# Five reorderings in a two-layer trunk kernel: attention fills, exponentials, query split, last sums, first low parts

## The chip, the cores and the metric

One core of a Trainium2 chip runs the whole kernel in one launch. The metric is the device time of one execution in microseconds; three executions of the kernel before took 386.45, 386.90 and 387.45 us, median 386.9. Below, PE is the matmul engine (TensorE), DVE is VectorE, ACT is ScalarE, POOL is GpSimd and SP is the engine that issues most DMAs.

## The reference

A decoder trunk of two layers over 256 tokens of width 1024, batch 1, all in fp32. Layer 0 is a gated DeltaNet (8 heads); its normalised output feeds shared keys and values and layer 1, a sparse attention with 16 query heads and three branches:

```python
for i in range(N_A_LAYERS):            # layer 0
    x = layer_norm(alpha * x + gated_deltanet_mixer(x, ...))
kv = x @ s_w_kv                        # one shared set: compressed, selected, window
for j in range(N_B_LAYERS):            # layer 1
    q, z, gate = split(x @ b_w_in)     # 1024, 3072, 48 columns
    o_b = softmax(q k_b) v_b           # for each of the three branches b
    y = sum_b sigmoid(gate)_b * o_b * silu(z)_b
    x = layer_norm(alpha * x + y @ b_w_out)
```

With 256 tokens every selection block is taken and the window covers everything, so the two halves of the tokens differ only in how many keys they see.

## The kernel before

Every fp32 product is made of three passes in a rounded fp32 format: high part by high part, high by low, low by high (`fm_part`, L215 to L217; `tm_part`, L233 to L235). The weights come as 512 KB tiles in the order they are used. Each tile is cast to its high part on ACT (L181) and its low part is the difference, on POOL (L185); `presplit` and `get` run some tiles ahead. The names say which weight: `wqkv` is layer 0's input projection, `bq`, `bz` and `bo` are layer 1's query, gate path and output projections; `hi_bz_6` is the high part of the seventh tile of `bz`.

The order of instructions on each engine is the order in which the program writes them: nothing reorders. Three devices set it. `defer(n, f)` puts a piece of work into a list and `step()` emits what has come due. `fills` is a list of small groups of projection matmuls; `fill(n)` takes n of them, so they stand on PE between pieces that wait for other engines. `merges` holds the transposes of finished heads that the output projection reads.

Start (L319 ff.): the tokens' transposed matrix `xT` arrives in four parts. ACT casts a part to `xh`, DVE subtracts for `xl`, and PE multiplies with the first weight chunk, `hi_first` and `lo_first`, whose low parts come from POOL (L322).

Queries: `q_done` rotates a block of queries, `q_split` (L1216) splits it into high and low parts (`hlq`, cast on ACT L1047, difference on DVE L1048), `q_post` transposes on PE into `qtp` and defers the copy to `qT` on ACT (L1224). Two matmul results `gq` give the three gates (`gates`, L1309 ff.: an exponential on ACT, four small instructions on DVE that leave `gt`). `gq` stands in one of the two score banks.

Attention (loop at the end of `trunk`, L1497 ff.): 24 units. A unit of the first token half (t0, named by its first head, such as 012) holds two heads; one of the second half (t1, such as 18) holds one. The string `UNITS` is their order; `FA` and `FB` say how many fill groups stand at two places of each unit. Per unit i: scores on PE; maxima on DVE (at once for t0 units until merges begin, else after `step()`); the copy of the transposed exponentials of the unit before (`probs`, ACT); `step()`, which emits the sums `total` (DVE, L1418 to L1422) and gate paths; FA fills; merges; weight splits; exponentials of unit i on ACT; readout of unit i-1 on PE into an `op` bank; FB fills; transposes of unit i on PE. The gate path of a `bz` block is a tanh on ACT (`th`, L1236) and a product on DVE (`zz`, L1237).

Tail: for the second token half the output projection is made in 256-wide pieces; `done` (L1454) calls `ln_part` (scaled residual plus projection, and statistics, on DVE), then `ln_affine` (L926): mean on DVE, the inverse root on POOL (L922, L923), two affine passes on DVE (L939, L942) and the output DMA.

Of the kernel before, what the change touches and what calls it, by code (L numbers as in the profile page):

```python
# [9 lines left out]
F32 = mybir.dt.float32  # L10
# [3 lines left out]
ALU = mybir.AluOpType  # L14
# [20 lines left out]

FIRST = (1, 2)

UNITS = "001010101101101101111111"
FA = "3113111011210212044211123"
FB = "0211121311122110212111000"  # L40

PRE, TAIL = 4, 2
NEG = -1e30
# [50 lines left out]
def trunk(ctx: ExitStack, tc: tile.TileContext, I: dict, out: bass.AP):  # L94
# [151 lines left out]
    def fill(n, low=True):  # L246
        for _ in range(n):
            step()
            if fills:
                fills.pop(0)()  # L250
            if low:
                lower()
# [66 lines left out]
    def split_first(c):  # L319
        h, l = splits[order[0]]  # L320
        S.copy(h[:, c], first[:, c])
        G.tensor_tensor(l[:, c], first[:, c], h[:, c].bitcast(F32), op=ALU.subtract)  # L322

    splits[order[0]] = tuple(ring.tile([P, 1024], F32R, tag=f"w{i}", name=f"{i}_first", bufs=NSPL) for i in ("hi", "lo"))
    state["s"] = 1
# [3 lines left out]
        PE.matmul(wps[:, 0:256], warm[:, 0:P], warm, start=True, stop=True)  # L329
    ps0 = pjb("pv0")  # L330
    w0 = [i.rearrange("p (k f) -> p k f", k=8) for i in splits[order[0]]]
    for q in range(5):
        if q < 4:
            c = slice(2 * q, 2 * q + 2)
            if q in FIRST:
                split_first(slice(FIRST.index(q) * 512, FIRST.index(q) * 512 + 512))
            for c in [c] if q < 2 else [slice(kt, kt + 1) for kt in (2 * q, 2 * q + 1)]:
                S.copy(xh[:, c, :], xT[:, c, :])
                V.tensor_tensor(xl[:, c, :], xT[:, c, :], xh[:, c, :].bitcast(F32), op=ALU.subtract)
        if q:  # L340
            for kt in range(2 * q - 2, 2 * q):
                for x in (xh, xl):
                    PE.matmul(gps[0:32, T:2 * T], wbs[:, kt, :], x[:, kt, :], start=x is xh and kt == 0,
                              stop=x is xl and kt == 7)
                    PE.matmul(ps0[:, 0:T], w0[0][:, kt, :], x[:, kt, :], start=x is xh and kt == 0, stop=False)
        if q == 2:
            for kt in range(4):
                PE.matmul(ps0[:, 0:T], w0[1][:, kt, :], xh[:, kt, :], start=False, stop=False)
# [559 lines left out]
    def ln_part(t, w, lo, ps, xin, dst):  # L908

        if lo == 0:  # L910
            stt[w, t] = [sm.tile([P, 4, 6], F32, tag="st", name=f"st_{w}{t}"), 0]
        st, n = stt[w, t]
        cc = slice(lo, lo + ps.shape[-1])
        V.scalar_tensor_tensor(dst[:, cc], xin[:, cc], SQRT2, ps, op0=ALU.mult, op1=ALU.add)
        V.bn_stats(st[:, n, :], dst[:, cc])
        stt[w, t][1] += 1

    def ln_mean(t, w):
# [6 lines left out]

    def ln_affine(t, w, b, dst, store=None, src=None):  # L926
        mv = ln_mean(t, w)
        if src:

            for c in range(2):  # L930
                V.scalar_tensor_tensor(src[c], src[c], mv[:, 0:1], lnp[w][:, c * 512:c * 512 + 512],
                                       op0=ALU.subtract, op1=ALU.mult)
            for c in range(2):
                cc = slice(c * 512, (c + 1) * 512)
                V.scalar_tensor_tensor(dst[:, cc], src[c], mv[:, 1:2], lnp[b][:, cc], op0=ALU.mult, op1=ALU.add)
            return
        for c in range(2):
            cc = slice(c * 512, (c + 1) * 512)
            V.scalar_tensor_tensor(dst[:, cc], dst[:, cc], mv[:, 0:1], lnp[w][:, cc], op0=ALU.subtract, op1=ALU.mult)  # L939
        for c in range(2):  # L940
            cc = slice(c * 512, (c + 1) * 512)
            V.scalar_tensor_tensor(dst[:, cc], dst[:, cc], mv[:, 1:2], lnp[b][:, cc], op0=ALU.mult, op1=ALU.add)  # L942
            if store:
                store(cc)
# [313 lines left out]
    add_pairs(48)  # L1258
    S.copy(wgs[:, :, 0:48], wg)
    G.tensor_tensor(wgs[:, :, 48:96], wg, wgs[:, :, 0:48].bitcast(F32), op=ALU.subtract)  # L1260
    fill(1)
    r = q_split()
    fill(1)
    compressed_v()
    for i in range(4):
        if i:
# [115 lines left out]
    def probs(u):  # L1382
        t, h = u
        PT = PTT[u] = wk.tile([P, 2, 2, P], F32, tag="ra", name=f"PT{t}{h}", bufs=6)
        S.copy(PT.rearrange("p a b c -> p (a b c)"), TP[u])  # L1385
        if t == 0 or h % 2:
            h -= h % 2 * t
            PCT[t, h] = pct[len(PCT) % 2]
            S.copy(PCT[t, h][0:32, :], S_[u][0:32, 1, 272:400])
# [53 lines left out]
    def bo_unit(t, c, part):  # L1443
        if part == 0:
            pb_[t, c] = [(sbank(f"pbl{c}{f}")[:, 0] if c else pjb(f"pbl{c}{f}")) for f in range(2)] if t else pjb(f"pbo{c}{t}")
        if t == 0 and c == 1 and part == 1:
            for nm in ("blw", "blb"):
                load_ln(nm, ring.tile([P, D], F32, tag="raw", name=nm, bufs=NRAW))
        x = x1[:, t, :]

        def store(cc):
            nc.sync.dma_start(out[t * P:(t + 1) * P, cc], x[:, cc])

        def done(lo, ps):  # L1454
            ln_part(t, "blw", lo, ps, x, x)
            if lo + ps.shape[-1] == D:
                (ln_affine if t else ln_affine_aside)(t, "blw", "blb", x, store)

        if t == 1:

            for f in range(2):
                ps = pb_[t, c][f][:, 0:256]
                tm_part(ps, ("bo", 4 * c + part), part, t, *bT, cols=slice(256 * f, 256 * f + 256))
                if part == 3:
                    done(512 * c + 256 * f, ps)
            return
        tm_part(pb_[t, c], ("bo", 4 * c + part), part, t, *bT)
        if part == 3:
            defer(1, lambda: done(512 * c, pb_[t, c]))
# [25 lines left out]
    for i in range(n + 1):  # L1495
        if i < n:
            scores(units[i])  # L1497
        first = i < n and units[i][0] == 0 and not merges
        if first:

            maxima(units[i])
        if i:
            probs(units[i - 1])
        step()
        if i < n and not first:
            maxima(units[i])
        fill(int(FA[i]))
        advance()
        presplit()
        if i < n:  # L1510
            exps(units[i])
        if i:
            t, h = units[i - 1]
            if t == 0:
                readout(t, h)
                if h == 14:
                    cnt["t0"] = 1
                    merges += [lambda: merge0(0), lambda: merge0(1)] + ready
            else:

                if (units[i - 2] if h % 2 else units[i]) == (1, h ^ 1):
                    readout(t, h - h % 2, h % 2)
                elif h % 2:
                    readout(t, h - 1)
                if h % 4 == 3:
                    (merges if cnt["t0"] else ready).append(lambda g_=h // 4: merge1(g_))
        fill(int(FB[i]))
        if i < n:
            transposes(units[i])
# [79 lines left out]
```

## Time and profile before

| | |
|---|---|
| median of three executions | 386.9 us |
| the profiled execution | 388.53 us, its span 386.8 us |
| PE busy | 374.7 us, 97% of the span |
| DVE, ACT, POOL busy | 58%, 57%, 64% |
| mean granted PE clock | 0.993 of full |
| chain that ended last | 90% PE, 3% DMA, 2% DVE |

The profile comes from one execution, and its span leaves out 1.7 us of that execution's time. PE's share on the chain says that nearly all of the time is spent with PE at work, so the rows to look for are the few in which PE stands idle and the one that released it.

### The profile page before, as it was taken

To read this page: it belongs to the slowest core of one execution; us is meant where nothing else is said; L and a number is where in the kernel's file an instruction comes from. 1 tells how busy PE (TensorE), PEld (TensorE's weight loads), DVE (VectorE), ACT (ScalarE), POOL (GpSimd) and SP (SyncE) were. 2 spreads that over 40 slices of the span, in tenths; PEclk is the share of its full clock that TensorE was granted. 3 is DMA by queue.
4 is the path that set the end of the run, shared out by engine and by line. 5 is a ranking of instruction groups with operands and counts; after the bars stand their busy time and mean duration, and the time that the engine had idled before them with its cause. 6 is when DMAs were issued, how large, how long until landed. Compare 5 with 4: busy or idle time off the path is not lost.

```text
span 386.8 us, 7558 instructions
## 1 busy us (share of the span) xinstructions
PE 374.7 (97%) x2870; PEld 332.9 (86%) x2870; DVE 223.6 (58%) x591; ACT 220.4 (57%) x433; POOL 247.1 (64%) x157
## 2 busy tenths in 40 slices
PE   8899999999999999999999999999999999999991
PEld 6899999999888987888897878888888888878991
DVE  2777876588642543656542545754557456677726
ACT  4687785546854543535563567675664757456410
POOL 5499999837456747895854997474736547209051
PEclk9999999999999999999999999999999999999997
DMA  6776749845433316384545854433516143301011
GB/s 223 292 218 208 268 158 297 228 167 143 148 109 112 110 54 200 128 287 147 169 158 166 297 195 159 164 111 109 173 45 218 55 153 113 117 3 54 3 54 54
DMA packets 23476, 58.68 MB, mean 152 GB/s; under 512 B 6672, under 2 KB 9232, under 8 KB 23312
## 3 DMA queue, kind: packets, MB, share of 16 engines
q1 hardware_dynamic: 23232, 58.13, 45.1%
q8 instruction: 22, 0.36, 0.4%
q14 instruction: 14, 0.11, 0.1%
q10 hardware_dynamic: 144, 0.07, 0.1%
q0 software_dynamic: 64, 0.01, 0.0%
HBM read 55.96 MB, written 2.23 MB: 150 GB/s over the span
## 4 chain that ended last, share of the span: by engine, by line
PE 90%; DMA 3%; DVE 2%; POOL 1%; ACT 1%; issue 1%; POOLq 0%; SPq 0%; DVEq 0%
PE pbz L235 6%; PE pbz L233 6%; PE pbz L234 6%; PE op L1407 4%; PE s L1336 3%; PE ptp L1378 3%; PE pwz L233 2%; PE pk L217 2%; PE pwo L235 2%; PE pq L216 2%; PE pq L215 2%; PE pq L217 2%; PE pk L215 2%; PE pk L216 2%; PE pwo L234 2%; PE pwo L233 2%
## 5 line engine op out<-in xcount | busy, mean ns | idle before, releaser
L185 POOL TENSOR_TENSOR lo_bz<-raw_bz,hi_bz 128x1024 fp32r<-128x1024 f32 x24 | 56.8, 2392 | 36.2 <-ACT hi_bz L181 19.6
L185 POOL TENSOR_TENSOR lo_wqkv<-raw_wqkv,hi_wqkv 128x1024 fp32r<-128x1024 f32 x22 | 52.5, 2406 | 7.9 <-ACT hi_wqkv L181 6.1
L233 PE MATMUL pbz<-hi_bz,x1h 128*128 128x512 f32 x96 | 38.7, 403 | 0.0
L235 PE MATMUL pbz<-lo_bz,x1h 128*128 128x512 f32 x96 | 37.8, 394 | 0.0
L234 PE MATMUL pbz<-hi_bz,x1l 128*128 128x512 f32 x96 | 37.6, 392 | 0.0
L185 POOL TENSOR_TENSOR lo_bo<-raw_bo,hi_bo 128x1024 fp32r<-128x1024 f32 x8 | 18.9, 2387 | 21.7 <-ACT hi_bo L181 16.9
L185 POOL TENSOR_TENSOR lo_skv<-raw_skv,hi_skv 128x1024 fp32r<-128x1024 f32 x12 | 28.4, 2397 | 4.2 <-PE pskv L235 4.2
L185 POOL TENSOR_TENSOR lo_wz<-raw_wz,hi_wz 128x1024 fp32r<-128x1024 f32 x8 | 19.4, 2438 | 16.0 <-ACT hi_wz L181 10.6
L181 ACT CAST hi_bz<-raw_bz 128x1024 fp32r<-128x1024 f32 x24 | 25.3, 1052 | 2.5 <-POOL wgs L1260 1.6
L185 POOL TENSOR_TENSOR lo_bq<-raw_bq,hi_bq 128x1024 fp32r<-128x1024 f32 x8 | 19.1, 2393 | 11.6 <-ACT hi_bq L181 7.2
L185 POOL TENSOR_TENSOR lo_wo<-raw_wo,hi_wo 128x1024 fp32r<-128x1024 f32 x8 | 18.9, 2385 | 11.9 <-ACT hi_wo L181 11.9
L1385 ACT COPY PT<-ptp 128x512 f32<-128x512 f32 x24 | 14.1, 588 | 21.2 <-PE ptp L1378 21.2
L181 ACT CAST hi_wqkv<-raw_wqkv 128x1024 fp32r<-128x1024 f32 x22 | 22.8, 1043 | 2.4 <-DMA raw_wqkv<-in_wqkv 2.4
L235 PEld LDWEIGHTS pbz<-lo_bz,x1h 128*128 128x128 f32 x96 | 18.0, 188 | 4.3 <-POOL lo_bz L185 0.2
L234 PEld LDWEIGHTS pbz<-hi_bz,x1l 128*128 128x128 f32 x96 | 18.1, 188 | 2.8
L233 PEld LDWEIGHTS pbz<-hi_bz,x1h 128*128 128x128 f32 x96 | 18.1, 188 | 2.8
L1369 ACT ACTIVATE pt<-s,mx 128x256 f32<-128x256 f32 x32 | 13.4, 471 | 10.9 <-DVE mx L1352 8.7
L217 PE MATMUL pk<-xh,lo_wqkv 128*128 128x256 f32 x64 | 18.2, 285 | 0.9 <-POOL lo_wqkv L185 0.9
L215 PE MATMUL pk<-xh,hi_wqkv 128*128 128x256 f32 x64 | 18.6, 290 | 0.0
L215 PE MATMUL pq<-xh,hi_wqkv 128*128 128x256 f32 x64 | 18.5, 289 | 0.0
L216 PE MATMUL pk<-xl,hi_wqkv 128*128 128x256 f32 x64 | 18.1, 283 | 0.0
L217 PE MATMUL pq<-xh,lo_wqkv 128*128 128x256 f32 x64 | 18.1, 283 | 0.0
(362 smaller groups left out, 1257.9 us busy)
## 6 DMA issues: line engine op xcount, KB each, us to landing
raw_bz<-in_bz SPq DMA_DIRECT2D x24, 512.0 KB, 3.3
raw_wqkv<-in_wqkv SPq DMA_DIRECT2D x23, 512.0 KB, 4.4
raw_skv<-in_skv SPq DMA_DIRECT2D x12, 512.0 KB, 3.3
raw_wz<-in_wz SPq DMA_DIRECT2D x8, 512.0 KB, 3.9
raw_wo<-in_wo SPq DMA_DIRECT2D x8, 512.0 KB, 3.6
raw_bq<-in_bq SPq DMA_DIRECT2D x8, 512.0 KB, 3.6
raw_bo<-in_bo SPq DMA_DIRECT2D x8, 512.0 KB, 3.3
raw_w<-in_w SPq DMA_DIRECT2D x4, 512.0 KB, 3.3
```

The lines of the kernel that those rows point to most:

```text
L181: S.copy(h, r)
L185: e.tensor_tensor(l, r, h.bitcast(F32), op=ALU.subtract)
L215: PE.matmul(ps[:, 0:T], wh[:, kt, :], ah[:, kt, :], start=kt == 0, stop=False)
L216: PE.matmul(ps[:, 0:T], wh[:, kt, :], al_[:, kt, :], start=False, stop=False)
L217: PE.matmul(ps[:, 0:T], wl[:, kt, :], ah[:, kt, :], start=False, stop=kt == 7)
L233: PE.matmul(ps, ah[:, kt, tt], wh[:, k4, cols], start=kt == 0, stop=False)
L234: PE.matmul(ps, al_[:, kt, tt], wh[:, k4, cols], start=False, stop=False)
L235: PE.matmul(ps, ah[:, kt, tt], wl[:, k4, cols], start=False, stop=kt == 7)
L1336: PE.matmul(sp[:, j, 0:n], lq, kk[:, hh // 4, c0:c0 + n], start=i == 0, stop=i == 1)
L1369: S.activation(pt[:, :, b, :], s4[:, :, b, :], AF.Exp, bias=mx[:, b:b + 1])
L1385: S.copy(PT.rearrange("p a b c -> p (a b c)"), TP[u])
L1407: PE.matmul(o3[:, r, 1 + b, :], PT[:, j, b, :], vt_[:, b, j, g_, :], start=j == 0, stop=j == 1)
```

## The change

Five parts. (1) `UNITS`, `FA` and `FB` are new tables: the t0 units stand at places 0, 1, 4, 7, 8, 12, 16 and 17 instead of 0, 1, 3, 5, 7, 10, 13 and 16, and the fills are dealt more evenly. (2) In the attention loop the exponentials move up: ahead of `step()` for t0 units until merges begin, and ahead of `presplit()` for the others (one fill group goes behind the merge when there is one). (3) The first `q_split` moves ahead of a fill. (4) In the tail the first half of the second token half's last sums stays in its two PSUM banks; the first affine pass is then three instructions, two of 256 columns from the banks and one of 512. (5) The two low parts of the first chunk move from POOL to DVE, between the subtractions for `xl`.

```diff
--- before.py
+++ after.py
@@ -35,9 +35,9 @@
 
 FIRST = (1, 2)
 
-UNITS = "001010101101101101111111"
-FA = "3113111011210212044211123"
-FB = "0211121311122110212111000"
+UNITS = "001101100111011100111111"
+FA = "3112121111111111111222223"
+FB = "0111111111111111101001000"
 
 PRE, TAIL = 4, 2
 NEG = -1e30
@@ -319,7 +319,8 @@
     def split_first(c):
         h, l = splits[order[0]]
         S.copy(h[:, c], first[:, c])
-        G.tensor_tensor(l[:, c], first[:, c], h[:, c].bitcast(F32), op=ALU.subtract)
+
+        return lambda: V.tensor_tensor(l[:, c], first[:, c], h[:, c].bitcast(F32), op=ALU.subtract)
 
     splits[order[0]] = tuple(ring.tile([P, 1024], F32R, tag=f"w{i}", name=f"{i}_first", bufs=NSPL) for i in ("hi", "lo"))
     state["s"] = 1
@@ -329,14 +330,17 @@
         PE.matmul(wps[:, 0:256], warm[:, 0:P], warm, start=True, stop=True)
     ps0 = pjb("pv0")
     w0 = [i.rearrange("p (k f) -> p k f", k=8) for i in splits[order[0]]]
+    low_first = []
     for q in range(5):
         if q < 4:
             c = slice(2 * q, 2 * q + 2)
             if q in FIRST:
-                split_first(slice(FIRST.index(q) * 512, FIRST.index(q) * 512 + 512))
+                low_first.append(split_first(slice(FIRST.index(q) * 512, FIRST.index(q) * 512 + 512)))
             for c in [c] if q < 2 else [slice(kt, kt + 1) for kt in (2 * q, 2 * q + 1)]:
                 S.copy(xh[:, c, :], xT[:, c, :])
                 V.tensor_tensor(xl[:, c, :], xT[:, c, :], xh[:, c, :].bitcast(F32), op=ALU.subtract)
+            if q % 2:
+                low_first.pop(0)()
         if q:
             for kt in range(2 * q - 2, 2 * q):
                 for x in (xh, xl):
@@ -911,8 +915,9 @@
             stt[w, t] = [sm.tile([P, 4, 6], F32, tag="st", name=f"st_{w}{t}"), 0]
         st, n = stt[w, t]
         cc = slice(lo, lo + ps.shape[-1])
-        V.scalar_tensor_tensor(dst[:, cc], xin[:, cc], SQRT2, ps, op0=ALU.mult, op1=ALU.add)
-        V.bn_stats(st[:, n, :], dst[:, cc])
+        y = ps if dst is None else dst[:, cc]
+        V.scalar_tensor_tensor(y, xin[:, cc], SQRT2, ps, op0=ALU.mult, op1=ALU.add)
+        V.bn_stats(st[:, n, :], y)
         stt[w, t][1] += 1
 
     def ln_mean(t, w):
@@ -925,7 +930,7 @@
 
     def ln_affine(t, w, b, dst, store=None, src=None):
         mv = ln_mean(t, w)
-        if src:
+        if src and not store:
 
             for c in range(2):
                 V.scalar_tensor_tensor(src[c], src[c], mv[:, 0:1], lnp[w][:, c * 512:c * 512 + 512],
@@ -934,9 +939,11 @@
                 cc = slice(c * 512, (c + 1) * 512)
                 V.scalar_tensor_tensor(dst[:, cc], src[c], mv[:, 1:2], lnp[b][:, cc], op0=ALU.mult, op1=ALU.add)
             return
-        for c in range(2):
-            cc = slice(c * 512, (c + 1) * 512)
-            V.scalar_tensor_tensor(dst[:, cc], dst[:, cc], mv[:, 0:1], lnp[w][:, cc], op0=ALU.subtract, op1=ALU.mult)
+        for c, y in enumerate(src):
+            cc = slice(c * 256, (c + 1) * 256)
+            V.scalar_tensor_tensor(dst[:, cc], y, mv[:, 0:1], lnp[w][:, cc], op0=ALU.subtract, op1=ALU.mult)
+        cc = slice(512, 1024)
+        V.scalar_tensor_tensor(dst[:, cc], dst[:, cc], mv[:, 0:1], lnp[w][:, cc], op0=ALU.subtract, op1=ALU.mult)
         for c in range(2):
             cc = slice(c * 512, (c + 1) * 512)
             V.scalar_tensor_tensor(dst[:, cc], dst[:, cc], mv[:, 1:2], lnp[b][:, cc], op0=ALU.mult, op1=ALU.add)
@@ -1258,9 +1265,8 @@
     add_pairs(48)
     S.copy(wgs[:, :, 0:48], wg)
     G.tensor_tensor(wgs[:, :, 48:96], wg, wgs[:, :, 0:48].bitcast(F32), op=ALU.subtract)
-    fill(1)
     r = q_split()
-    fill(1)
+    fill(2)
     compressed_v()
     for i in range(4):
         if i:
@@ -1452,9 +1458,14 @@
             nc.sync.dma_start(out[t * P:(t + 1) * P, cc], x[:, cc])
 
         def done(lo, ps):
-            ln_part(t, "blw", lo, ps, x, x)
+
+            inb = t == 1 and lo < 512
+            ln_part(t, "blw", lo, ps, x, None if inb else x)
             if lo + ps.shape[-1] == D:
-                (ln_affine if t else ln_affine_aside)(t, "blw", "blb", x, store)
+                if t:
+                    ln_affine(t, "blw", "blb", x, store, [p[:, 0:256] for p in pb_[1, 0]])
+                else:
+                    ln_affine_aside(t, "blw", "blb", x, store)
 
         if t == 1:
 
@@ -1501,14 +1512,19 @@
             maxima(units[i])
         if i:
             probs(units[i - 1])
+        if first:
+            exps(units[i])
         step()
         if i < n and not first:
             maxima(units[i])
-        fill(int(FA[i]))
+
+        k = 1 if merges else 0
+        fill(int(FA[i]) - k)
         advance()
+        fill(k)
+        if i < n and not first:
+            exps(units[i])
         presplit()
-        if i < n:
-            exps(units[i])
         if i:
             t, h = units[i - 1]
             if t == 0:
```

The number of instructions stays the same on PE, ACT and SP; DVE gets four more and POOL one row fewer.

ACT at the split of the first query block, before (`hlq000` is the high part of the first block's first half, `kh` the compressed keys', `wgs` the gate weights):

```order
L1259 CAST wgs_2832<-wg_2360 128x8x48 [waits DMAHW2_49]
L1188 CAST kh_2288<-kcp_2825 128x4x16 [waits DVE_49]
L181 CAST hi_bq_7_2846<-raw_bq_7_2737 128x1024 [waits DMAHW6_49,Pool_49]
L181 CAST hi_bz_0_2852<-raw_bz_0_2739 128x1024 [waits DMAHW7_49,Pool_49]
L1047 CAST hlq000_2862<-pbq00_2705 128x4x64
L181 CAST hi_bz_1_2883<-raw_bz_1_2745 128x1024 [waits DMAHW0_49,Pool_49]
```

and now:

```order
L1266 CAST wgs_2832<-wg_2360 128x8x48 [waits DMAHW2_49]
L1054 CAST hlq000_2836<-pbq00_2705 128x4x64 [waits DVE_49]
L1195 CAST kh_2288<-kcp_2825 128x4x16 [waits DVE_49]
L181 CAST hi_bq_7_2849<-raw_bq_7_2737 128x1024 [waits DMAHW6_49,Pool_49]
L181 CAST hi_bz_0_2855<-raw_bz_0_2739 128x1024 [waits DMAHW7_49,Pool_49]
L181 CAST hi_bz_1_2883<-raw_bz_1_2745 128x1024 [waits DMAHW0_49,Pool_49]
```

The cast of `hlq000` moved up past the keys' cast and two weight casts.

ACT at the opening of the attention, before (`qT1` are the last two copies of transposed queries, `gq` the gates' exponential, `pt00` and `Pc00` the exponentials of the first unit, `th00` the tanh of the first gate block):

```order
L181 CAST hi_bz_6_3049<-raw_bz_6_2908 128x1024 [waits DMAHW5_49,Pool_49]
L1224 CAST qT1_2696<-qtp110_3059 128x4x128 [waits PE_49]
L1224 CAST qT1_2696<-qtp111_3064 128x4x128 [waits PE_49]
L1310 ACT_TABLE_LOAD
L1310 ACTIVATE gq_3069<-gq_3069 128x96 [waits PE_49]
L181 CAST hi_bz_7_3090<-raw_bz_7_2935 128x1024 [waits DMAHW6_49,Pool_49]
L1236 ACTIVATE th00_3101<-pbz00_3004 128x512 [waits PE_49]
L1365 ACTIVATE pt00_3117<-s00_3072,mx00_3077 128x128 [waits DVE_49,Activation_49]
L1365 ACTIVATE pt00_3117<-s00_3072,mx00_3077 128x128
L1366 ACTIVATE Pc00_3118<-s00_3072,mx00_3077 128x16
```

and now:

```order
L181 CAST hi_bz_6_3049<-raw_bz_6_2908 128x1024 [waits DMAHW5_49,Pool_49]
L1371 ACT_TABLE_LOAD [waits DVE_49,PE_49]
L1371 ACTIVATE pt00_3081<-s00_3072,mx00_3077 128x128 [waits Activation_49]
L1371 ACTIVATE pt00_3081<-s00_3072,mx00_3077 128x128
L1372 ACTIVATE Pc00_3082<-s00_3072,mx00_3077 128x16
L1371 ACTIVATE pt00_3081<-s00_3072,mx00_3077 128x128 x2
L1372 ACTIVATE Pc00_3082<-s00_3072,mx00_3077 128x16
L1231 CAST qT1_2696<-qtp110_3059 128x4x128
L1231 CAST qT1_2696<-qtp111_3064 128x4x128
L1316 ACTIVATE gq_3069<-gq_3069 128x96
L181 CAST hi_bz_7_3098<-raw_bz_7_2935 128x1024 [waits DMAHW6_49,Pool_49]
```

The table load and the six exponentials of unit 00 moved ahead of both copies and of the gates' exponential; the load now waits for DVE and PE.

DVE around the maxima `mx014` of the last t0 unit, before (`op` and `rc` of one number are one sum, `total`):

```order
L1349 TENSOR_TENSOR s18_3968<-s18_3968,cb_2284 128x256 [waits PE_49,Activation_49]
L1350 TENSOR_TENSOR s18_3968<-s18_3968,cb_2284 128x16 [waits DVE_49]
L1351 TENSOR_REDUCE mx18_3976<-s18_3968 128x2 [waits DVE_49]
L1352 TENSOR_REDUCE mx18_3976<-s18_3968 128x1
L1237 SCALAR_TENSOR_TENSOR zz3_3808<-th41_3993,pbz41_3896 128x512 [waits Activation_49]
L1345 TENSOR_TENSOR s014_4030<-s014_4030,cb_2284 128x2x272 [waits PE_49]
L1346 TENSOR_REDUCE mx014_4035<-s014_4030 128x4 [waits DVE_49]
L1347 TENSOR_REDUCE mx014_4035<-s014_4030 128x2
L1418 RECIPROCAL op16_4014<-op16_4014 128x6
```

and now:

```order
L1351 TENSOR_TENSOR s012_3962<-s012_3962,cb_2284 128x2x272 [waits PE_49,Activation_49]
L1352 TENSOR_REDUCE mx012_3967<-s012_3962 128x4 [waits DVE_49]
L1353 TENSOR_REDUCE mx012_3967<-s012_3962 128x2
L1244 SCALAR_TENSOR_TENSOR zz1_3560<-th50_3982,pbz50_3878 128x512 [waits Activation_49]
L1424 RECIPROCAL op18_3945<-op18_3945 128x6 [waits PE_49]
L1425 TENSOR_TENSOR rc18_4003<-op18_3945,gt_2977 128x6 [waits DVE_49]
L1426 TENSOR_TENSOR op18_3945<-op18_3945,zz3_3869 128x6x64 [waits DVE_49]
L1427 TENSOR_TENSOR op18_3945<-op18_3945,rc18_4003 128x6x64 [waits DVE_49]
L1428 TENSOR_REDUCE zz3_3869<-op18_3945 128x128 [waits DVE_49]
L1351 TENSOR_TENSOR s014_4021<-s014_4021,cb_2284 128x2x272 [waits PE_49]
L1352 TENSOR_REDUCE mx014_4026<-s014_4021 128x4 [waits DVE_49]
L1353 TENSOR_REDUCE mx014_4026<-s014_4021 128x2
```

Before, a gate product stood directly ahead of `mx014`; now a gate product and the five instructions of the sum of 18 do, and the maxima of 012 stand ahead of those.

## Rows read from the trace of the kernel before

**Rows 1.** The page, part 1: busy time of each engine, share of the span, instructions.
```profile
PE 374.7 (97%) x2870; PEld 332.9 (86%) x2870; DVE 223.6 (58%) x591; ACT 220.4 (57%) x433; POOL 247.1 (64%) x157
```

**Rows 2.** Waits of TensorE: line waited for, total us, times, longest.
```profile
PE pk L217 <- POOL lo_wqkv L185: 0.9, 1, 0.9
...
PE qtp L1223 <- DVE hlq L1048: 0.5, 1, 0.5
```

**Rows 3.** Timeline of PE, opening: start us, us, instruction [idle before <-releaser].
```profile
240.28 0.37 PE L1336 MATMUL s<-kh,qT 128*128 128x272 f32 x1
...
240.87 0.40 PE L233 MATMUL pbz<-hi_bz,x1h 128*128 128x512 f32 x1
...
244.98 0.60 PE L1378 MATMUL ptp<-ident,pt 128*128 128x128 f32 x4
...
245.45 0.37 PE L1336 MATMUL s<-kh,qT 128*128 128x272 f32 x1
```

**Rows 4.** Timeline of PE, last attention units.
```profile
337.56 0.91 PE L1378 MATMUL ptp<-ident,pt 128*128 128x128 f32 x4
...
340.02 2.00 PE L1407 MATMUL op<-vtok,PT 128*128 128x65 f32 x16 [0.16 <-DVE zz L1422]
...
344.59 1.11 PE L1407 MATMUL op<-vtok,PT 128*128 128x65 f32 x8 [0.39 <-DVE zz L1422]
```

**Rows 5.** Timeline of DVE after the last matmul.
```profile
380.39 1.42 DVE L939 SCALAR_TENSOR_TENSOR x<-x,mv_blw,blw 128x512 f32<-128x512 f32 x2
382.26 1.42 DVE L942 SCALAR_TENSOR_TENSOR x<-x,mv_blw,blb 128x512 f32<-128x512 f32 x2 [0.46 <-POOL mv_blw L923]
```

**Rows 6.** Chain of waits, 0 to 20 us: start us, us, what.
```profile
6.78 7.41 DMA raw_wqkv<-in_wqkv
...
15.34 2.40 POOL lo_wqkv L185
```

**Rows 7.** Chain of waits, 218 to 246 us.
```profile
221.55 1.06 ACT hi_bz L181
```

**Rows 8.** Timeline of ACT, opening of the attention.
```profile
239.68 1.07 ACT L1224 CAST qT<-qtp 128x512 fp32r<-128x512 f32 x2 [0.20 <-PE qtp L1223]
240.78 1.28 ACT L1310 ACT_TABLE_LOAD   x1
242.07 0.23 ACT L1310 ACTIVATE gq<-gq 128x96 f32<-128x96 f32 x1
...
243.16 0.60 ACT L1236 ACTIVATE th<-pbz 128x512 f32<-128x512 f32 x1
243.64 0.63 ACT L1365 ACTIVATE pt<-s,mx 128x128 f32<-128x128 f32 x2
...
244.30 0.65 ACT L1365 ACTIVATE pt<-s,mx 128x128 f32<-128x128 f32 x2
```

**Rows 9.** Timeline of DVE, opening of the attention.
```profile
241.07 0.73 DVE L1345 TENSOR_TENSOR s<-s,cb 128x544 f32<-128x544 f32 x1 [2.56 <-PE s L1336]
...
242.55 0.26 DVE L1311 TENSOR_SCALAR gq<-gq 128x96 f32<-128x96 f32 x1
...
243.93 0.24 DVE L1315 TENSOR_SCALAR gt<-gq,cb 128x16 f32<-128x16 f32 x1
```

**Rows 10.** Timeline of DVE, last attention units.
```profile
337.18 0.69 DVE L1237 SCALAR_TENSOR_TENSOR zz<-th,pbz 128x512 f32<-128x512 f32 x1 [0.50 <-ACT th L1236]
337.78 0.20 DVE L1418 RECIPROCAL op<-op 128x6 f32<-128x6 f32 x1
...
339.41 0.56 DVE L1422 TENSOR_REDUCE zz<-op 128x128 f32<-128x384 f32 x1
```

**Rows 11.** Timeline of DVE, layer norm of the first layer.
```profile
155.67 1.42 DVE L931 SCALAR_TENSOR_TENSOR pwo<-pwo,mv_alw,lna 128x512 f32<-128x512 f32 x2
157.00 1.40 DVE L935 SCALAR_TENSOR_TENSOR x<-pwo,mv_alw,lna 128x512 f32<-128x512 f32 x2
```

**Rows 12.** Slice 381 to 382 us: busy of each engine, then granted clock.
```profile
381.00:382.00 1.00, 0.00 (x0) 0.00 (x0) 0.80 (x2) 0.00 (x0) 0.92 (x2) 0.82 0.00 0
```

## Prediction

> **What bounds the kernel now.** I read the page first, then what TensorE waits for, then the timelines of the three places the diff touches. TensorE (PE) is busy 374.7 of 386.8 us [rows 1]: anything that lets it start its next matmul earlier is worth its full length, anything that makes it wait costs its full length, and work on the other engines is free until PE stands. So the change can only remove waits of PE and the little that lies before its first and behind its last matmul, and has to be searched for waits it adds.
>
> The waits there are few. Near the start PE waits 0.9 us for one low part of a weight, ahead of the attention 0.5 us for the low part of the split queries [rows 2]. In the attention opening PE runs eighteen fill matmuls behind the first scores, then transposes, then the second unit's scores, without a gap [rows 3]. At the end of the attention it does stand: 0.16 and 0.39 us for the last step of a sum, and the four transposes that need 0.60 us in the opening take 0.91 there [rows 3, 4], because their second pair waits for an exponential. Counting such excess start to start, at some ten places of the same kind between 333.9 and 344.6 us, I get 2.1 us, of which these three rows show 0.9. After the last matmul Vector finishes the layer norm alone [rows 5].
>
> **Part 5, the start: 0.** With the low parts of the first chunk off POOL, the subtractions of x no longer share time with it and PE meets its early matmuls some tenths sooner. But the next thing PE needs is the low part of a projection weight: its DMA takes 7.41 us and lands at 14.19, ACT casts, POOL subtracts from 15.34 for 2.40 [rows 6]. None of the three is moved, so PE arrives sooner and waits longer than 0.9. Bounds: a gain of at most 0.9 would need the transfer to land earlier, and no DMA is issued earlier; a loss would need Vector's extra 1.3 us of subtraction to delay something. I take 0, with ±0.3.
>
> **Part 3, the queries' split: −0.54.** ACT casts hi_bz_0 for 1.06 us [rows 7] directly ahead of the first hlq, and PE then waits 0.5 (0.54 in its row's idle time) for Vector's half of that split [rows 2]. Now the cast of hlq stands two weight casts earlier, behind wgs; its input is long there. The wait goes. Next in line behind it are the matmuls of the query projection, whose weights are split already. What is pushed back 0.27 us is the key cast and two weight casts, consumed over 2 us later. Bounds: 0 to −0.6.
>
> **Part 2 in the opening: +2.70.** Here the move costs. In the row order ACT now does, behind the first maxima: table load, six exponentials of unit 00, then the two last qT copies, then the gates' exponential gq. Before, both copies and gq stood ahead. Nothing else on ACT can pass the table load, since it carries the wait. With the durations of [rows 8] and the times of [rows 3, 9]:
> - The maxima hand over at about 242.6 (the next Vector instruction starts at 242.55 [rows 9]). Before, the table load (1.28) had run from 240.78 beneath the copies' and maxima's time; now it starts at 242.65 and ends at 243.95.
> - Exponentials of a two-head unit take 1.31 from the first start to the last end (243.64 to 244.95): 245.26. The copies take 1.07: 246.33.
> - The transposes of unit 00 take the one transpose bank, which the second copy frees: 246.37 instead of 244.98, a wait of 1.39.
> - gq takes 0.23 and ends near 246.47. Vector's four gate instructions last 1.62 (242.55 to 244.17) and end at 248.1. The second unit's scores need the score bank in which gq stands (two banks, three users), so they start near 248.15 instead of 245.45 [rows 3].
>
> Thus PE stands 1.39 ahead of the transposes and 1.31 behind them, 2.70 in all. Nothing covers it: PE runs in order, and the eighteen matmuls that could have filled it are already spent at 244.98. Bounds: 1.4 if the gates end with the transposes, 2.9 with semaphore delays added.
>
> **Parts 1 and 2 in the rest: −2.1 and +3.0.** The new tables deal one or two fill groups (six matmuls, 4.11/3 = 1.37 us) to every unit, and leave no late unit without. The excess at the end goes: I count all 2.1 as gained. But they also move two-head units (t0) together to places 16 and 17, with only one group and one readout between the scores of the last, unit 014, and its transposes. Walk that place from the scores of 012 at time 0. Maxima start at +0.79 and take 1.55 (241.07 to the next row) [rows 9]; exponentials start a tenth later, at 2.46, and the next ACT work, th50, at 3.78 (0.60 [rows 8], its reader Vector released after 0.6). Then Vector runs zz50 (0.6 to its successor [rows 10]), then the sum of 18, 337.78 to 339.97 or 2.19 [rows 10], and only then the maxima of 014: near 7.2. Those give 8.75, exponentials end near 10.2. PE meanwhile: scores 0.58, group, readout 1.04, group, transposes 0.47, scores 0.58, group, readout 1.04, which is 7.8 (scores and transposes from [rows 3]; a readout is the 1.11 of [rows 4] less what lies under its successor). It waits some 2.3; I take 1.9, since a few of these ends overlap their successors' starts by a tenth. The same walk at the other units gives 0.43 (a readout behind the sum two units back), 0.3 (maxima behind a zz), 0.37 (a copy behind two weight casts) and 0.6 (exponentials behind a copy of merged heads, a th and a cast), rounded together to 3.0 after 0.6 off for those that a wait just before already covers. Bounds: 0.8, if Vector is ahead at each place because PE was held just before, to 4.5.
>
> **Part 4, the tail: −0.5.** Today Vector's first affine pass reads and writes SBUF and the second starts 1.87 us after it (380.39 to 382.26), held 0.46 by POOL's power [rows 5]. In the first layer's norm, whose operand lies in PSUM, the same pair stands 1.33 apart and POOL is no wait [rows 11]. Two of the three new instructions read PSUM, so I expect that distance and a little more, for the third instruction: 1.37, a gain of 0.5. Bounds 0 to −0.55. The sums and statistics of the first half move to PSUM in equal number and size: the 512-wide affine pair takes 1.42 from PSUM as from SBUF [rows 5, 11], so no price. [...]
>
> **Sum.** +2.70 +3.0 −0.54 −2.1 −0.5 +0 = **+2.6 us**. The profiled execution took 388.53 (span 386.8), 1.6 over the median of 386.9; added to its own time the sum gives 391.1, and against the median, which is what is forecast, **389.5 us**. A measurement of this kernel tells about 0.3% (1.16 us) from no change.
>
> **Rivals.**
> - *Only the opening costs.* The late chains bind little (0.8) because Vector and ACT run ahead: 2.70+0.8−3.14 = +0.4, **387.3 us**, no change. For it: Vector is idle 42% of the span [rows 1]. Against it: at unit 014 the order itself serializes zz, sum and maxima, whatever the idle share.
> - *Faster.* The table load's wait isn't what it seems, or gq's bank is not what holds the second scores, so that the opening costs 1.4 at most and the late waits 0.5: 1.9−3.14 = −1.2, **385.7 us**. It decides when opening and late waits together stay under 3.14 − 1.16 = 1.98 us. Against it: two independent orders, ACT's and the bank's, would both have to be misread.
> - *The clock falls in the opening.* PE would stand 1.39 us, do 0.47 of transposes and stand 1.31. [...] Against it: the transposes break the stand into two, and no row shows the clock falling before PE's last matmul, though no wait there is longer than 0.9 [rows 2]. [...]
>
> **Chances and range.** Forecast (+1.2 to +4.4) 0.72, only the opening 0.15, clock 0.08, faster 0.05. So slower 0.80, no change 0.15, faster 0.05. The range runs from 387.2 (late waits at their lower bound) to 391.3 (late waits at 4.5 with the gains short by a little), leaving out the faster case, the clock case and a strip of each end.
>
> **What would show it.** In the new profile: the table load near 242.1 on ACT (0.54 earlier than above) with the copies and gq behind the exponentials; PE idle about 1.4 ahead of the first transposes, released by ACT's copy, and about 1.3 ahead of the second scores, released by Vector's gates; a wait near 2 us of the transposes of 014 on an exponential; no wait for hlq; an unchanged arrival of lo_wqkv near 17.7; the last pair of affine passes about 1.4 apart. The prediction is wrong if PE's waits behind the opening come to less than 1 us in total, or if the second scores don't wait.

## The result and the profile after

The changed kernel took 391.81 us in the median of six executions (390.02 to 396.58), the kernel before 387.02; the ratio is 1.0117 (95% interval 1.0077 to 1.0156), some 4.5 us. The forecast was 389.5 with a range that ended at 391.3: the direction was right, the size nearly twice as large, and the time lies outside the range. The shortest executions lie half a microsecond over the sum; it is the others, up to 6 us longer, that carry the median out. The longest counts as a slow execution, which the ratio leaves out; the median of the other five is 391.19, but three more runs of the same kernel, below, gave 391.75 to 392.32.

TensorE's work is the same, so its busy time hardly moved (before: [rows 1]):

```profile
PE 375.3 (97%) x2870; PEld 332.3 (86%) x2870; DVE 223.2 (57%) x594; ACT 219.2 (56%) x433; POOL 243.9 (63%) x155
```

Its waits, as in [rows 2] (line waited for, total us, times, longest):

```profile
PE ptp L1384 <- ACT qT L1231: 1.4, 1, 1.4
PE s L1342 <- DVE gt L1321: 1.1, 1, 1.1
...
PE op L1410 <- DVE zz L1428: 0.8, 2, 0.4
PE ptp L1384 <- ACT pt L1371: 0.5, 1, 0.5
PE gps L372 <- DVE ba L357: 0.4, 1, 0.4
```

The wait for hlq is gone, and so, here, is that for the first low weight. New are the two of the opening, the second query copy (1.4) and the gates (1.1). The place itself, on PE, and what ACT did (before: [rows 3, 8]):

```profile
238.00 0.37 PE L1342 MATMUL s<-kh,qT 128*128 128x272 f32 x1
...
244.22 0.66 PE L1384 MATMUL ptp<-ident,pt 128*128 128x128 f32 x4 [1.35 <-ACT qT L1231]
...
246.12 0.36 PE L1342 MATMUL s<-kh,qT 128*128 128x272 f32 x1 [1.13 <-DVE gt L1321]
```

```profile
240.44 1.28 ACT L1371 ACT_TABLE_LOAD   x1 [3.23 <-DVE mx L1353]
...
243.06 1.11 ACT L1231 CAST qT<-qtp 128x512 fp32r<-128x512 f32 x2
244.01 0.30 ACT L1316 ACTIVATE gq<-gq 128x96 f32<-128x96 f32 x1
```

```profile
245.74 0.24 DVE L1321 TENSOR_SCALAR gt<-gq,cb 128x16 f32<-128x16 f32 x1
```

ACT loads its table at 240.44, when the maxima are there, works through the exponentials, copies the queries at 243.06 and does gq at 244.01, as the new order says; Vector's last gate instruction ends at 245.98, and the second scores start at 246.12. From first to second scores PE takes 8.12 us where it took 5.17 [rows 3]: +2.95.

At unit 014 the chain of Vector that the prediction walked stands in the trace, a product, the sum of 18, then the maxima (before: [rows 9, 10]):

```profile
329.80 0.69 DVE L1244 SCALAR_TENSOR_TENSOR zz<-th,pbz 128x512 f32<-128x512 f32 x1 [2.11 <-ACT th L1243]
330.41 0.20 DVE L1424 RECIPROCAL op<-op 128x6 f32<-128x6 f32 x1
...
332.51 0.72 DVE L1351 TENSOR_TENSOR s<-s,cb 128x544 f32<-128x544 f32 x1
...
333.88 0.18 DVE L1353 TENSOR_REDUCE mx<-s 128x2 f32<-128x32 f32 x1
```

```profile
332.74 1.08 PE L1410 MATMUL op<-vtok,PT 128*128 128x65 f32 x8 [0.37 <-DVE zz L1428]
...
334.60 1.27 PE L1384 MATMUL ptp<-ident,pt 128*128 128x128 f32 x4 [0.50 <-ACT pt L1371]
```

The product starts at 329.80, the sum at 330.41, the maxima at 332.51, and the transposes that need the exponentials start 0.50 late and take 1.27 instead of 0.60: 1.2 lost, not 1.9. The readout ahead of them waits 0.37 for the sum as well.

The tail after the last matmul, Vector and then POOL (before: [rows 5]):

```profile
379.81 0.41 DVE L919 SCALAR_TENSOR_TENSOR pbl<-x,pbl 128x256 f32<-128x256 f32 x1
380.26 0.43 DVE L920 BATCH_NORM_STATS2 st_blw<-pbl 128x6 f32<-128x256 f32 x1
380.61 0.40 DVE L919 SCALAR_TENSOR_TENSOR x<-x,pbl 128x256 f32<-128x256 f32 x1
381.05 0.43 DVE L920 BATCH_NORM_STATS2 st_blw<-x 128x6 f32<-128x256 f32 x1
...
382.59 0.88 DVE L944 SCALAR_TENSOR_TENSOR x<-pbl,mv_blw,blw 128x256 f32<-128x256 f32 x2
383.38 0.74 DVE L946 SCALAR_TENSOR_TENSOR x<-x,mv_blw,blw 128x512 f32<-128x512 f32 x1
384.04 1.41 DVE L949 SCALAR_TENSOR_TENSOR x<-x,mv_blw,blb 128x512 f32<-128x512 f32 x2
```

```profile
382.64 0.22 POOL L927 TENSOR_SCALAR mv_blw<-mv_blw 128x1 f32<-128x1 f32 x1 [6.70 <-DVE mv_blw L926]
```

First to second affine pass is 1.45 us, from 1.87. The sum into PSUM (379.81) takes 0.41, the one into SBUF (380.61) 0.40; both read PSUM. The statistics are the same instruction from either memory: 0.43 from PSUM (380.26) and 0.43 from SBUF (381.05). POOL's first small step takes 0.22 beside Vector's pass from PSUM.

The start, before (Vector, then POOL) and now (Vector), at the second part of x:

```profile
7.44 1.28 DVE L339 TENSOR_TENSOR xl<-xT,xh 128x512 fp32r<-128x512 f32 x1 [0.43 <-ACT xh L338]
```

```profile
6.89 1.29 POOL L322 TENSOR_TENSOR lo_first<-raw_first,hi_first 128x512 fp32r<-128x512 f32 x1 [2.34 <-ACT hi_first L321]
```

```profile
7.30 0.69 DVE L341 TENSOR_TENSOR xl<-xT,xh 128x512 fp32r<-128x512 f32 x1 [0.55 <-ACT xh L340]
```

One trace is one execution, and the start differs from one to the next: the first matmul that needs a POOL-made low weight stands at 17.78 in the trace of before, at 16.29 here, and between 16.2 and 18.8 in the traces below, as the token matrix and the first weights arrive. So I compare stretches behind it. From it to the first scores: 222.50 before, 221.71 now (-0.79). First to second scores: +2.95. From there to the end of the last matmul: 133.49 and 135.00 (+1.51). From that to the end of the span: 7.88 and 7.47 (-0.41). Sum: +3.3 us.

### The profile page after: what moved, and what is told of

It reads as the page before. It is cut to its first block, busy times and chain, and to the rows that moved or that the text cites. A ratio compares the mean times of both kernels' runs of the same rounds, so it can differ in the third digit from the quotient of the medians.

```text
span 388.6 us, 7550 instructions
## 1 busy us (share of the span) xinstructions
PE 375.3 (97%) x2870; PEld 332.3 (86%) x2870; DVE 223.2 (57%) x594; ACT 219.2 (56%) x433; POOL 243.9 (63%) x155
## 5 line engine op out<-in xcount | busy, mean ns | idle before, releaser
L216 PE MATMUL pq<-xl,hi_wqkv 128*128 128x256 f32 x64 | 18.1, 283 | 0.0
```

Of the source, the lines that this page charges most:

```text
L216: PE.matmul(ps[:, 0:T], wh[:, kt, :], al_[:, kt, :], start=False, stop=False)
```

## The experiments

Two theories stood. *Waits:* the change costs the waits seen in the trace, and the executions spread for a reason of the start. *Clock:* while PE stands in those waits the granted clock falls in some executions, and the matmuls behind run at the lower level: 0.50 in the traces below that show a fall, against 1.00. Each execution lists its span and mean granted clock. Of the first six of the change, three had a clock of 0.994 to 0.996 and spans of 388.3 to 389.2 us, three 0.988 to 0.991 and 390.5 to 393.8.

**The change again.** No edit; with the result above, four runs in all.

> The changed kernel once more, for its spread and a second trace. Clock theory: in part of the executions TensorE's granted clock falls in or behind the two stands of the attention opening, so the times spread again over more than 3 us (390 to 396) and go with the mean granted clock of each execution; a trace of one of the longer ones shows a stretch behind 244 us at the lower level. Waits theory (the price is the waits alone, about 2.5 us in the opening and 1.5 behind it): the times lie within 1.5 us of each other, about 390, with no such stretch; or they spread for another reason, the start's DMA.

Measured 392.32 us against 387.65 (ratio 1.0117, 1.0092 to 1.0141); the traced execution was the shortest, with no stretch at the lower clock behind the start.

> The changed kernel a third time. So far 5 of its 12 executions had a mean granted clock of 0.991 or less, with spans of 390.5 to 393.8 us, and 7 had 0.994 or more, with spans of 388.3 to 390.3. Clock theory: again some 4 in 10 at 0.991 or less, a median near 391.5, and if the trace is of such an execution, a stretch at the lower level behind 244 us. Waits theory: no relation, no such stretch.

Measured 391.75 (1.0127, 1.0097 to 1.0156). The span of this trace is 1.3 us longer than that of the first, and it shows a fall of the clock at unit 014, to 0.50 from 337 to 339 us:

```profile
332.98 1.08 PE L1410 MATMUL op<-vtok,PT 128*128 128x65 f32 x8 [0.36 <-DVE zz L1428]
...
334.84 1.27 PE L1384 MATMUL ptp<-ident,pt 128*128 128x128 f32 x4 [0.50 <-ACT pt L1371]
...
335.98 0.43 PE L1342 MATMUL s<-kh,qT 128*128 128x272 f32 x1
...
336.87 0.63 PE L233 MATMUL pbz<-hi_bz,x1h 128*128 128x512 f32 x1
...
338.57 0.63 PE L234 MATMUL pbz<-hi_bz,x1l 128*128 128x512 f32 x1
```

The waits of 0.36 and 0.50 are those of the first trace, but the first score matmul, at 335.98, takes 0.43 instead of 0.37, and the fill matmuls from 336.87 take 0.63 instead of 0.39. From the second scores to the last matmul this trace takes 136.05 us, the first one 135.00: a fall here costs 1.05.

> The changed kernel on the chip of the next two, for comparison: a median near 391.7, some 4 in 10 executions at a mean clock of 0.991 or less.

Measured 392.30 (1.0115, 1.0083 to 1.0147). In this trace the clock falls in the opening, in the middle of the first fill group behind the second scores (0.79 from 246 to 248 us, 0.50 from 248 to 250):

```profile
244.38 0.66 PE L1384 MATMUL ptp<-ident,pt 128*128 128x128 f32 x4 [1.35 <-ACT qT L1231]
...
246.28 0.36 PE L1342 MATMUL s<-kh,qT 128*128 128x272 f32 x1 [1.14 <-DVE gt L1321]
...
246.85 0.39 PE L233 MATMUL pbz<-hi_bz,x1h 128*128 128x512 f32 x1
...
247.43 0.63 PE L235 MATMUL pbz<-lo_bz,x1h 128*128 128x512 f32 x1
...
248.28 0.63 PE L234 MATMUL pbz<-hi_bz,x1l 128*128 128x512 f32 x1
```

From the second scores to the last matmul it takes 136.52 us where the first trace took 135.00: this fall costs 1.5. In all, 12 of 24 executions of the change had a mean clock of 0.991 or less, their median 393.1, the others' 391.0; of the kernel before, 4 of 80. The mean is a rough sign: both traced falls have a mean of 0.992, and it does not say where the clock fell. At 0.992 or less it is 14 of 24 against 7 of 80.

**Opening repaired.** Only the first unit's exponentials go back:

```diff
-        if first:
+        if first and i:
             exps(units[i])
...
-        if i < n and not first:
+        if i < n and not (first and i):
             exps(units[i])
```

> The change, but the first unit's exponentials stand where they stood before, behind both query copies and the gates' exponential. Both theories: the stands of 1.35 and 1.13 us go, no wait for the second query copy, none for the gates. Waits theory: 391.8 less 2.9 gives 388.9 and the spread of times stays. Clock theory: the lower clock goes too, another 1.5 to 4 us, so 385 to 387.5, and the spread falls under 1.5 us.

Measured 388.60 (1.0031, 1.0016 to 1.0046). Both waits are gone from the trace. The time fell by 3.2 to 3.7 us; that this is more than the 2.95 of waits is not clear of the intervals. The median lies where the waits theory had it (388.9) and over the 387.5 of the clock theory. The spread did not fall under 1.5 either: 2 of 12 executions had the low clock, and the traced one shows it at the start, where the second part of the token matrix came late and PE stood 1.4 us for its cast; the granted clock is 0.50 from 12 to 14 us. That is a third place where the clock fell behind a wait, of which I had not thought.

**PE kept busy in the opening.** The same waits, but PE multiplies by zeros meanwhile, into the accumulation that is open:

(`none` is a tile of zeros, `state["pj"]` the bank of the latest fill group; the lines that set them are left out here)

```diff
...
+    def keep(m):
+        for _ in range(m):
+            PE.matmul(state["pj"][:, 0:256], none, warm, start=False, stop=False)
...
+        if i == 1:
+            keep(9)
         if i < n:
             scores(units[i])
...
+        if i == 0:
+            keep(11)
         if i < n:
             transposes(units[i])
```

> The change with 11 small matmuls by zeros ahead of the first transposes and 9 ahead of the second scores, added into the accumulation that stands open there (they add zero): TensorE waits for the same copies and gates, but works meanwhile. Waits theory: same time as the change, 390 to 392, same spread. Clock theory: first transposes and second scores start as late as in the change, but the clock stays at the upper level, so about 389 to 390, with a spread under 1.5 us.

Measured 390.41 (1.0076, 1.0060 to 1.0092), all five executions within 0.8 us. The median lies in the range of the waits theory and above the clock theory's 389 to 390; the small spread is the clock theory's, and against the same runs of the kernel before the change took 392.32. First and second scores are 8.11 us apart, as in the change, and PE is busy in between with the clock up (columns: stretch, length, PE, its weight loads, DVE, ACT and POOL busy, granted clock):

```profile
242.00:244.00 2.00, 2.00 (x15) 1.53 (x14) 0.00 (x0) 2.00 (x8) 0.00 (x0) 1.00 0.86 246
244.00:246.00 2.00, 1.89 (x17) 1.36 (x14) 1.38 (x4) 2.00 (x5) 0.49 (x1) 1.00 0.05 18
...
248.00:250.00 2.00, 2.00 (x15) 1.84 (x14) 0.99 (x4) 1.26 (x6) 0.00 (x0) 1.00 0.43 154
```

> The change with zeros multiplied in the two stands of the opening, a second time; 0 of 5 executions had a clock of 0.991 or less so far. Clock theory: again none or one, median near 390.4, a spread under 1.5 us, 1 to 2 us under the change on the same chip. Waits theory: the same median and spread as the change.

Measured 390.58 (1.0101, 1.0070 to 1.0133): five executions from 390.45 to 390.67 and one of 394.65 at a clock of 0.990. With the first five that is 1 of 11 at the low clock, against 12 of 24; the waits theory had no difference.

**The stand made longer.** The first unit's exponentials are done twice:

```diff
         if first:
             exps(units[i])
+        if i == 0:
+            exps(units[i])
```

> The change with the first unit's six exponentials done twice, so that the stand ahead of the first transposes grows by 1.3 us to about 2.7 and everything behind it starts 1.3 later. Waits theory: 1.3 over the change's shortest executions, 391.3 to 391.7, trace at the upper clock throughout. Clock theory: the longer stand lets the clock fall in most executions, so a median of 393 to 396, mean granted clock 0.99 or less, and the trace shows a stretch at the lower level starting between 242 and 250 us.

Measured 394.06 (1.0177, 1.0141 to 1.0212), four of four at 0.991 or less, as the clock theory had it. The waits grew by 1.3, the time by some 2, of four executions alone. In the trace PE does nothing from 246 to 248, and from 250 to 252 the granted clock is 0.50:

```profile
246.00:248.00 2.00, 0.00 (x0) 0.00 (x0) 0.00 (x0) 2.00 (x9) 0.00 (x0) 1.00 0.15 61
...
250.00:252.00 2.00, 2.00 (x7) 1.81 (x8) 1.16 (x2) 0.13 (x2) 1.57 (x1) 0.50 0.00 0
```

This trace is the longest of the four and fell at the start too (0.50 from 12 to 14 us, behind a wait of 1.5 for the token matrix), so its 396.39 is not the opening's alone.

**Which of the two places.** Zeros at unit 014 alone (3 ahead of the readout of 012, 5 ahead of the transposes), and at both:

```diff
+        if i == 17:
+            keep(3)
         if i:
             t, h = units[i - 1]
...
+        if i == 17:
+            keep(5)
         if i < n:
             transposes(units[i])
```

> The change with 3 multiplications by zeros ahead of the readout of 012 and 5 ahead of the transposes of 014, where one trace of the change shows the lower clock; the opening stands as in the change. If the clock falls mostly at 014: 390.0 to 390.6, no execution at 0.991 or less but for a late start. If it falls mostly in or through the opening: like the change, 391 to 392.

Measured 391.81 (1.0108, 1.0073 to 1.0143), four of six at the low clock, and in the trace it falls in the opening, at the second scores (0.59 from 246 to 248 us, behind waits of 1.35 and 1.13). The stretch behind the second scores is 1.5 us longer than in the first trace, as in the third repeat. Filling 014 alone changes nothing that six executions show.

> Zeros at both places. Clock theory: the waits alone are left, 390.0 to 390.5, spread under 1.5 us. Were the extra time of the change something else than the clock: as the change.

Measured 390.90 (1.0082, 1.0056 to 1.0109), none of six at the low clock. So the opening brings most of the falls; that 014 brings some rests on the one trace above. With the stands filled the change costs what its waits cost: 3.2 us by the ratio, 3.3 by the stretches of the first trace.

**The opening alone, in the kernel before.**

```diff
+        if i == 0:
+            exps(units[i])
         step()
...
-        if i < n:
+        if 0 < i < n:
             exps(units[i])
```

> The kernel before with one edit: the first unit's exponentials ahead of the deferred copies and the gates' exponential. Waits theory: 387.0 plus 2.5 to 2.9, 389.5 to 389.9, with a spread like before's (1 us). Clock theory: 1.5 to 4 us more, a median of 391 to 394, and a spread of over 3 us.

Measured 390.80 (1.0087, 1.0068 to 1.0106), 3.4 us over before. First to second scores take 8.12 as in the change: the waits are the edit's alone. Between the theories it does not decide: no execution had 0.991 or less, three had 0.992, the traced one, one of these three, fell nowhere, and the time lies between the two expectations.

**The other parts.** The kernel before with split, tail and start; and the same without the start:

```diff
...
-        G.tensor_tensor(l[:, c], first[:, c], h[:, c].bitcast(F32), op=ALU.subtract)
+        return lambda: V.tensor_tensor(l[:, c], first[:, c], h[:, c].bitcast(F32), op=ALU.subtract)
...
```

> The kernel before with the query split, the tail and the start of the change; tables and attention loop as before. Prediction's terms: -0.54 (split), -0.45 (tail), 0 (start): 1.0 under before, 386.6. Rival for the start: the late weight in the profile of before was one execution's transfer, and usually the first chunk's low parts do hold matmuls up: another 0.5 to 1 us, 385.6 to 386.1.

> The same without the start's edit. Prediction's terms: 386.6, the same as with it. Rival for the start: 0.5 to 1 us longer than the kernel with it.

Measured 386.62 (0.9968, 0.9951 to 0.9985) and 386.60 (0.9973, 0.9959 to 0.9987), before 387.71. Split and tail give 1.1, the start nothing.

**Tables and moved exponentials.** The new tables on top of those three parts with the old loop, and the change with its opening repaired and the old tables:

> The kernel before with split, tail and start of the change (386.6 measured) and the new tables, the attention loop as before, so no exponential is moved. If the order of units makes the waits behind the opening (a product and a sum ahead of the maxima of 014, readouts behind sums), most of the 2.0 us by which the change with its opening repaired (388.6) lies over 386.6 is there: 388 to 389. If the moved exponentials make them: 386.6.

Measured 388.20 against 387.13 (1.0020, 1.0008 to 1.0032): by the ratios the tables cost 2.0 us over the kernel without them (0.9968). Its longest waits behind the opening stand behind unit 014, 0.65 us for an exponential and 0.55 for Vector ahead of the transposes at 342 and 347 us. The exponentials moved in later units cost some 0.4 more by the ratios (1.0031), which is inside the intervals and not in the traces: from second scores to last matmul 134.73 with them, 135.00 without.

> The change with the first unit's exponentials back and with the old tables; later exponentials stay moved up. Tables theory (the new order of units brings 3.7 us of waits and removes 2.1): about 1.6 under the kernel with the new tables, so 387.0, or less where the earlier exponentials shorten the old waits at the end. Rival (the moved exponentials themselves hold back casts and tanhs): no difference, 388.6.

Measured 391.11 (1.0092, 1.0066 to 1.0118), where 387.0 was expected. My theory left out what the moved exponentials push back there. PE's longest waits:

```profile
PE pbz L235 <- POOL lo_bz L185: 1.7, 1, 1.7
PE pbl L233 <- DVE x L919: 1.2, 1, 1.2
```

POOL had stood 3.08 us for a gate weight's high part from ACT, where the cast comes behind the moved exponentials; PE then stood 1.7 us for the low part, and the clock fell behind that too (0.50 from 262 to 264 us). Near the end it stood 1.2 for Vector. Neither the tables nor the moved exponentials are a gain alone, nor together.

**A version that beats both.** Split, tail and start, loop and unit order of before, and two fill groups kept for the units that merge heads (the fours and twos near the end of the old tables ask for groups that the list no longer holds):

```diff
-FA = "3113111011210212044211123"
-FB = "0211121311122110212111000"
+FA = "3112111011210211011111123"
+FB = "0211111311112110200111000"
```

> Split, tail and start of the change, the loop and the unit order of before, and two fill groups kept back for the two units that merge the first half's heads (one from unit 18, one from unit 19). Waits there of 0.2 to 0.6 us (1.3 in all before) should go: 385.4 to 385.8 against 386.6. If the units that give the groups stand instead, no gain: 386.6 or more.

Measured 384.45 against 387.13 (0.9939, 0.9918 to 0.9960): 2.4 us under before by the ratio, and 1.1 under the kernel with the three parts alone, whose interval overlaps this one; the traces have 131.71 against 133.45 from the second scores to the last matmul. Expected were 385.4 to 385.8. All the waits of PE that the view lists are in the start:

```profile
PE warm L330 <- PEq L1610: 0.8, 1, 0.8
PE gps L347 <- ACT xh L340: 0.5, 1, 0.5
PE gps L372 <- DVE ba L357: 0.4, 1, 0.4
PE pv L349 <- ACT hi_first L321: 0.2, 1, 0.2
```

## Why the prediction was wrong

- **Part 5, the start, 0:** right, by two kernels that differ in it alone. Vector's subtraction of x falls from 1.28 us, beside POOL's low part, to 0.69. The reason that I gave for the 0 is not shown: neither of the two traces lists a wait for the first low weight, which PE takes at 16.79 and 17.03, and its arrival was not the fixed 17.7 that I named. Why the start gains nothing stays open.
- **Part 3, the split, -0.54:** the trace has -0.79 up to the first scores. **Part 4, the tail, -0.5:** -0.41 in the trace. The sum of the two, -1.04, was measured as -1.1.
- **The opening, +2.70:** both waits at their place, with the releasers named, 1.35 and 1.13 us of idle time. In all it is 2.95: the transposes start 1.52 later than before, not 1.39, and the second scores another 1.43, not 1.31, from small delays. The table load starts 2.44 us behind the first scores instead of 2.37, and the second scores 0.14 behind the last gate instruction instead of 0.05.
- **The rest, -2.1 and +3.0:** the balance was +0.9, the trace has +1.51, so it was mis-sized by some 0.6. The kernel of the last experiment, with no listed wait behind its start, takes 131.71 us over this stretch. Against it the kernel before has at least 1.78 to give and the change loses at least 3.29: the loss was sized too low, and whether the gain was 2.1 stays open. At 014 it was 1.2 and a wait of 0.37 at the readout, not 1.9. The walk also took 1.55 for the maxima where its rows give 1.48, twice.
- **The sum** of waits was +2.6. With PE's stands filled it was measured as +2.9, +3.9 and +3.2 in three runs of two kernels; these three took 390.4 to 390.9 us, inside the range.
- **The step that failed** is the chance of the third rival. I set the clock at 0.08, because the transposes break the stand into two, and let the range end below it. The runs show a low mean clock in half of the executions; in the traces the clock falls behind the two broken waits, and at 014 behind waits of 0.36 and 0.50. The start that the change also moved does not explain it: of 43 executions of the four kernels that have it without the opening's waits (opening repaired, the three parts, the tables, the later fills), 3 had 0.991 or less. The falls that were traced behind these waits cost 1.05 to 1.5 us each, and beside the kernels with filled stands the median of the change lies 1.2 to 1.9 higher. That 392 us, my estimate for this rival, was the result is in part luck: it was made of 389.5 and a guess of two to three microseconds for a fall, a term that no run shows; the runs show 390.4 to 390.9 and 1.2 to 1.9. The trace of before shows no fall ahead of its last matmul, 1.00 in every stretch of 2 us; behind its start PE's longest wait in it is 0.5 us [rows 2].

Open: why the same waits bring the clock down in one execution and not in the next, why the opening alone in the kernel before showed none at 0.991, and how much of the spread at full clock (388.3 to 390.3 us of span) is the start. Six of the 24 executions of the change also took 2.4 to 3.0 us more than their span, the others 1.7 to 2.0, and none of the 80 of the kernel before took 2.4; why is open too.

## What to carry to other kernels

A wait added to an engine that is otherwise never idle cost more here than its length: the two falls traced behind waits of 0.36 to 1.35 us took another 1.05 and 1.5 us, and 12 of 24 executions had the low mean clock. Price the matmuls behind such a wait at the lower clock as well, and as a likely case. When work is moved up on an engine that runs in order, write down everything it passes, with whom each of those frees, banks included; here a 0.23 us exponential [rows 8] held the scores, which waited 1.13 us. Judge the parts of a bundle one by one: two of five were worth 1.1 us, one nothing, and two cost over 5 together, while two groups kept for the place where the supply runs out gave about 1.

## What the runs showed of the hardware

The clock falls at some executions and not at others under waits that agree to a hundredth of a microsecond: 1.35 and 1.13 us in the first trace, which has no fall, and 1.35 and 1.14 in that of the third repeat. In the trace of the first repeat, without a fall either, the matmuls behind the opening ran at a granted clock of 1.00:

```profile
248.00:250.00 2.00, 2.00 (x15) 1.82 (x15) 0.98 (x5) 1.47 (x6) 0.00 (x0) 1.00 0.65 199
```

and in the trace of the third repeat, behind its waits, at 0.50:

```profile
248.00:250.00 2.00, 2.00 (x9) 1.71 (x8) 0.61 (x2) 1.27 (x6) 0.00 (x0) 0.50 0.57 197
```

With PE multiplying by zeros in the opening's waits, 16 of 17 executions kept a mean clock above 0.991, and the shortest times of their three runs, 389.98 to 390.45 us, are those of the four of the change, 390.02 to 390.49.
